# Transposing on VectorE instead of TensorE in a batched product x yᵀ: pair-packed casts, 32x32 block transposes and block-diagonal weights

## The chip, the cores and the metric

The kernel runs on one core of one Trainium2 chip. The metric is the device time of one execution in microseconds; the median of several runs is quoted. The profile of an execution covers a span that is about 2 us shorter than the device time. A run is called slow when it lies over 1.5% above the fastest of the same kernel.

In the profile lines PE is TensorE's matmuls, PEld its weight loads, DVE VectorE, ACT ScalarE and POOL GpSimd; q1 is the queue of the kernel's DMAs, q8 and q14 are the queues that the page calls "instruction". A packet of a load or an output is one contiguous row (the 24 loads of the kernel before, of 256 rows of 4 KB each, are 6144 packets of 4 KB).

## The reference

```python
batch, n_heads, seq_t, seq_s, channels = 8, 12, 512, 512, 64
# x: (8, 12, 512, 64) float32, y: (8, 12, 512, 64) float32
np.einsum('bhtc,bhsc->bhts', x, y)        # out: (8, 12, 512, 512) float32
```

There are 96 heads. Each is a product of a 512x64 and a 64x512 matrix. Inputs are 25.17 MB, the output is 100.66 MB: the kernel mostly writes.

## The kernel before

It takes 8 heads per group and has 12 groups. POOL casts the inputs to bf16, TensorE transposes them (128x128 against an identity), VectorE and ACT copy the transposes out of PSUM, TensorE multiplies with 64x64 weights, ACT and VectorE evict 128x1024 blocks into an output tile of 2 MB, and one DMA writes each tile. The parts that matter here:

```python
xv = x...rearrange("(g a p n) -> g p a n", a=2, p=P, n=R * C)   # rows of 4 KB, two per partition
lpool bufs=3, opool bufs=6 ...
def load(g):
    nc.sync.dma_start(ys..., yv[g]); nc.sync.dma_start(xs..., xv[g])
def prepare(g, made):                     # in steps, amid the matmuls of group g - 1
    ... nc.gpsimd.tensor_copy(b[:, rows], s[:, :, rows]...)     # 4 casts of 128x1024
    if g + AHEAD < NG: load(g + AHEAD)
    ... nc.tensor.transpose(pt[:, k, :], yb[...], ident)        # 32 per group
    ... nc.vector.tensor_copy(dst, src) / nc.scalar.activation(dst, src, COPY)
# cut: loops over groups, head pairs and k
for two in range(2):
    for h in range(2):
        nc.tensor.matmul(pm[h * 64:(h + 1) * 64, two, :], xT[...64 columns...], yT[...512 columns...])
if k % 2 == 0: nc.scalar.activation(ot[...], pm, COPY)
else:          nc.vector.tensor_copy(ot[...], pm)
# 2 MB per output DMA; at the two ends of the run in halves of 1 MB
nc.sync.dma_start(ov[g, 2 * a + pair], otf)
```

## Time and profile before

| | before |
|---|---|
| device time, median | 306.41 us (306.17 to 306.41, its first 3 runs) |
| span of the profile | 304.3 us |
| instructions on PE and PEld | 2304 |
| 16 KB instruction fetches (queue q8) | 9 |
| DMA packets of data | 6144 of 4 KB, 1024 of 8 KB, 5632 of 16 KB |
| last compute | 277.6 us |

The prediction below shows the main lines. Two more groups of that page are what the change removes (line, engine, operation, output and input, count; busy time and mean nanoseconds; idle time ahead of it and its releaser):

```profile
L126 PE MATMUL pm<-yT,xT 64*64 64x512 bf16 x768 | 164.0, 610 | 56.0 <-ACT ot L133 53.9
...
L82 PE MATMUL pt<-ident,yb 128*128 128x128 bf16 x192 | 23.7, 307 | 10.7 <-POOL yb L73 6.9
```

The second appears twice, for yb and xb. The page's chain of waits has PE in 23% of the span, most of that before 63 us, where PE is busy nearly all the time. But the DMA row is at 9 there too, and later the matmuls wait for ACT, and ACT for output DMAs. So this time should not set the end.

A word that the document uses throughout: each DMA leaves 16 completion increments in the trace (1216 for the 76 DMAs of the kernel before), and the page counts 16 DMA engines. One increment is read as the end of one engine's part; the times fit this, as 16 packets of 159 ns, a sixteenth of a load of 1 MB, take 2.54 us, and the first increments of two such loads are 2.56 us apart. The **spread** of a DMA is the time from its first increment to its last. It tells how far the slowest engine lags the fastest. No view of the profile prints it; it was computed from the increments in the trace.

### The profile page before, as it was taken

The numbers are of one execution on the slowest core, as the hardware profiler recorded it, in microseconds if no ns is written. First come the engines' busy times: TensorE is split into PE (matmuls) and PEld (weight loads), VectorE is DVE, ScalarE is ACT, GpSimd is POOL, SyncE is SP. The second block draws the span as 40 slices with busy tenths as digits, with TensorE's granted clock in tenths as the row PEclk, the third lists the DMA queues.
The fourth block names the chain that finished last, engine by engine and source line by source line (L and its number), as shares of the span: only waits on it lengthen the run. The fifth ranks groups of instructions, "written<-read, shape, count | busy, mean of one in ns | idle before, by whom it ended". The sixth has DMA issues, their size and how long they took to land.

```text
span 304.3 us, 2968 instructions
## 1 busy us (share of the span) xinstructions
PE 208.5 (69%) x1152; PEld 104.6 (34%) x1152; DVE 144.7 (48%) x120; ACT 119.4 (39%) x121; POOL 49.3 (16%) x54
## 2 busy tenths in 40 slices
PE   0899999999959538928946844893897797671000
PEld 0444344555425114513613522541453443330000
DVE  0456666567446435616525733743565664443000
ACT  1454645364445224624515512542364552522000
POOL 3773220400500310230050050031000000000000
PEclk9999999999999855555555655555555555555555
DMA  7999999999999999999999999999999999999992
GB/s 283 411 410 418 436 429 423 419 442 405 445 419 419 430 431 421 420 437 424 426 426 435 414 429 433 413 433 429 433 433 429 431 433 429 428 428 433 423 420 89
DMA packets 14031, 126.03 MB, mean 414 GB/s; under 512 B 1216, under 2 KB 1216, under 8 KB 7360
## 3 DMA queue, kind: packets, MB, share of 16 engines
q1 hardware_dynamic: 14016, 125.83, 98.2%
q8 instruction: 9, 0.15, 0.2%
q14 instruction: 6, 0.05, 0.0%
HBM read 25.17 MB, written 100.66 MB: 413 GB/s over the span
## 4 chain that ended last, share of the span: by engine, by line
DMA 60%; PE 23%; DVE 4%; ACT 2%; issue 1%; POOL 1%; SPq 0%; ACTq 0%
DMA out_dram<-ot 48%; PE pm L126 17%; DMA xs<-in_x_dram 12%; PE pt L82 3%; PE pt L96 3%; DVE ot L135 2%; ACT ot L133 2%; DVE xT L102 1%; POOL xb L73 1%; SPq L55 0%; ACTq L133 0%; SPq L140 0%; ACT xT L104 0%; SPq L56 0%
## 5 line engine op out<-in xcount | busy, mean ns | idle before, releaser
L126 PE MATMUL pm<-yT,xT 64*64 64x512 bf16 x768 | 164.0, 610 | 56.0 <-ACT ot L133 53.9
L135 DVE COPY ot<-pm 128x1024 f32<-128x1024 f32 x96 | 117.2, 1223 | 113.3 <-PE pm L126 57.3
L133 ACT ACTIVATE ot<-pm 128x1024 f32<-128x1024 f32 x96 | 95.1, 1023 | 113.7 <-DMA out_dram<-ot 81.2
L126 PEld LDWEIGHTS <-xT 64*64 64x64 bf16 x768 | 66.1, 150 | 131.2 <-issue 122.7
L73 POOL CAST yb<-ys 128x1024 bf16<-128x1024 f32 x24 | 24.3, 1040 | 140.5 <-DMA ys<-in_y_dram 94.7
L82 PE MATMUL pt<-ident,yb 128*128 128x128 bf16 x192 | 23.7, 307 | 10.7 <-POOL yb L73 6.9
L73 POOL CAST xb<-xs 128x1024 bf16<-128x1024 f32 x24 | 24.3, 1040 | 16.3 <-issue 6.9
L82 PEld LDWEIGHTS <-yb 128*128 128x128 bf16 x192 | 19.9, 143 | 20.3 <-issue 11.5
L96 PE MATMUL pt<-ident,xb 128*128 128x128 bf16 x192 | 24.9, 310 | 1.1 <-POOL xb L73 0.9
L96 PEld LDWEIGHTS <-xb 128*128 128x128 bf16 x192 | 19.1, 141 | 19.3 <-issue 17.8
L104 ACT ACTIVATE xT<-pt 128x1024 bf16<-128x1024 bf16 x12 | 12.3, 1024 | 32.9 <-PE pt L96 29.4
L102 DVE COPY xT<-pt 128x1024 bf16<-128x1024 bf16 x12 | 14.7, 1223 | 10.8 <-PE pt L96 9.4
L88 DVE COPY yT<-pt 128x1024 bf16<-128x1024 bf16 x12 | 14.6, 1216 | 8.9 <-PE pt L82 8.9
L90 ACT ACTIVATE yT<-pt 128x1024 bf16<-128x1024 bf16 x12 | 12.3, 1022 | 9.3 <-PE pt L82 7.7
L90 ACT ACT_TABLE_LOAD x1 | 1.3, 1283 | 0.7 <-PEq L155 0.7
masks.py:199 POOL TENSOR_SCALAR_AFFINE_SELECT ident<-ident 128x128 bf16<-128x128 bf16 x1 | 0.3, 292 | 0.1
masks.py:197 POOL MEMSET ident<- 128x128 bf16 x1 | 0.2, 204 | 0.3 <-POOLq L155 0.3
L155 POOL MEMSET const-float32-0.0<- 128x1 f32 x1 | 0.1, 98 | 0.2 <-issue 0.2
L155 POOL MEMSET const-bfloat16-1.0<- 128x1 bf16 x1 | 0.1, 101 | 0.0
L155 POOL MEMSET const-uint8-127<- 128x1 uint8 x1 | 0.1, 101 | 0.0
L155 POOL MEMSET const-float32-1.0<- 128x1 f32 x1 | 0.1, 98 | 0.0
## 6 DMA issues: line engine op xcount, KB each, us to landing
out_dram<-ot SPq DMA_DIRECT2D x44, 2048.0 KB, 28.3
ys<-in_y_dram SPq DMA_DIRECT2D x12, 1024.0 KB, 20.3
xs<-in_x_dram SPq DMA_DIRECT2D x12, 1024.0 KB, 22.2
out_dram<-ot SPq DMA_DIRECT2D x8, 1024.0 KB, 21.0
```

What stands on the lines that cost most here:

```text
L73: nc.gpsimd.tensor_copy(b[:, rows], s[:, :, rows].rearrange("p a r c -> p r a c"))
L82: nc.tensor.transpose(pt[:, k, :], yb[:, half * K + k].rearrange("p a c -> p (a c)"), ident)
L88: nc.vector.tensor_copy(dst, src)
L90: nc.scalar.activation(dst, src, COPY)
L96: nc.tensor.transpose(pt[:, k, :], xb[:, e * K + half * K // 2 + i].rearrange("p a c -> p (a c)"), ident)
L102: nc.vector.tensor_copy(dst, src)
L104: nc.scalar.activation(dst, src, COPY)
L126: nc.tensor.matmul(pm[h * 64:(h + 1) * 64, two, :], xT[a * C:(a + 1) * C, 2 * k + two, col:col + Q].rearrange("c n e -> c (n e)"), yT[a * ...
L133: nc.scalar.activation(ot[:, 2 * k:2 * k + 2, :], pm, COPY)
L135: nc.vector.tensor_copy(ot[:, 2 * k:2 * k + 2, :], pm)
L155: nc = _bacc.Bacc("TRN2", target_bir_lowering=False, num_devices=1)
```

## The change

Its intent is to take the transposes away from TensorE, and with them the copies out of PSUM. The casts arrange channel halves in partition blocks of 32 and pack two values per 32-bit element; VectorE transposes 32x32 blocks of such elements; weights become 128x128 blocks that are block-diagonal over two heads (the zeros are written once). Each partition now loads 8 KB in one piece, and every output is a DMA of 2 MB. Cut to its core:

```diff
-    xv = ....rearrange("(g a p n) -> g p a n", a=2, p=P, n=R * C)
-    ov = ....rearrange("(g a p n) -> g a p n", a=4, p=P, n=K * S)
+    xv = ....rearrange("(g p n) -> g p n", p=P, n=R * C)
+    ov = ....rearrange("(o u h q n) -> o h q u n", u=2, h=2, q=Q * E, n=K * S)
-    opool ... bufs=6
+    opool ... bufs=7
-            nc.gpsimd.tensor_copy(b[:, rows], s[:, :, rows].rearrange("p a r c -> p r a c"))
+    # six casts per half group on POOL, each of 32 or 64 partitions
+    cast(engines[n % len(engines)], xv2[(2 * ch + u) * D:(2 * ch + u + 1) * D, :, :, :, u], ...)
-            nc.tensor.transpose(pt[:, k, :], yb[...], ident)      # 384 in all, and 48 copies
+    nc.vector.transpose(xT..., xb...)                              # 24 of 128x1024 uint32
+    nc.vector.transpose(yT..., yb...)                              # 24 of 128x512 uint32
-    nc.tensor.matmul(pm[h * 64:(h + 1) * 64, two, :], <64 columns>, ...)      # 768
+    nc.tensor.matmul(pm[:, two, :], xT[:, k + two, h, :], yT[:, h * S:(h + 1) * S], ...)   # 384
+    if step == 12 and g + AHEAD < NG:
+        load(g + AHEAD)                                            # just ahead of the group's last tile
+    if k == 4: nc.vector.tensor_copy(...)                          # else ACT: 3 of 4 evictions
```

More of the change, by code (lines that the diff above doesn't have):

```diff
@@ L6 @@
 from concourse._compat import with_exitstack
-from concourse.masks import make_identity
 @with_exitstack
@@ L26 @@
     P = 128
-    G = 4
+    G = 8
     Q = P // G
     R = T // Q
-    NG = B * H // (2 * G)
-    K = R // 2
+    NG = B * H // G
+    K = 8
+    E = R // K
+    D = 32
     AHEAD = 3
@@ L34 @@
     bf16 = mybir.dt.bfloat16
+    u32 = mybir.dt.uint32
     COPY = mybir.ActivationFunctionType.Copy
-    assert C * 2 == P and S == T and R == 16
-    xv = x.rearrange("b h t c -> (b h t c)").rearrange("(g a p n) -> g p a n", a=2, p=P, n=R * C)
-    yv = y.rearrange("b h t c -> (b h t c)").rearrange("(g a p n) -> g p a n", a=2, p=P, n=R * C)
-    ov = out.rearrange("b h t s -> (b h t s)").rearrange("(g a p n) -> g a p n", a=4, p=P, n=K * S)
+    assert C == 2 * D and S == T and R == D and Q * 2 == D
@@ L42 @@
+    xv = x.rearrange("b h t c -> (b h t c)").rearrange("(g p n) -> g p n", p=P, n=R * C)
+    yv = y.rearrange("b h t c -> (b h t c)").rearrange("(g p n) -> g p n", p=P, n=R * C)
+    ov = out.rearrange("b h t s -> (b h t s)").rearrange(
+        "(o u h q n) -> o h q u n", u=2, h=2, q=Q * E, n=K * S
+    )
     const = ctx.enter_context(tc.tile_pool(name="const", bufs=1))
     lpool = ctx.enter_context(tc.tile_pool(name="lpool", bufs=AHEAD))
-    bpool = ctx.enter_context(tc.tile_pool(name="bpool", bufs=2))
@@ L45 @@
-    tpool = ctx.enter_context(tc.tile_pool(name="tpool", bufs=2))
-    opool = ctx.enter_context(tc.tile_pool(name="opool", bufs=6))
-    ptpool = ctx.enter_context(tc.tile_pool(name="ptpsum", bufs=2, space=bass.MemoryType.PSUM))
-    pmpool = ctx.enter_context(tc.tile_pool(name="pmpsum", bufs=3, space=bass.MemoryType.PSUM))
-    loaded = {}
+    ybpool = ctx.enter_context(tc.tile_pool(name="ybpool", bufs=2))
+    tpool = ctx.enter_context(tc.tile_pool(name="tpool", bufs=4))
+    opool = ctx.enter_context(tc.tile_pool(name="opool", bufs=7))
@@ L52, in load @@
+    pmpool = ctx.enter_context(tc.tile_pool(name="pmpsum", bufs=4, space=bass.MemoryType.PSUM))
+    loaded, made = {}, {}
+    zeroed = [const.tile([P, K * E * D], u32, name=f"xb{half}") for half in range(2)]
     def load(g):
-        xs = lpool.tile([P, 2, R, C], fp32)
-        ys = lpool.tile([P, 2, R, C], fp32)
-        nc.sync.dma_start(ys.rearrange("p a r c -> p a (r c)"), yv[g])
-        nc.sync.dma_start(xs.rearrange("p a r c -> p a (r c)"), xv[g])
+        xs = lpool.tile([P, R, C], fp32)
+        ys = lpool.tile([P, R, C], fp32)
+        nc.sync.dma_start(xs.rearrange("p r c -> p (r c)"), xv[g])
+        nc.sync.dma_start(ys.rearrange("p r c -> p (r c)"), yv[g])
@@ L57, in load @@
         loaded[g] = (xs, ys)
-    for g in range(AHEAD):
-        load(g)
-    ident = const.tile([P, P], bf16)
-    make_identity(nc, ident)
-    def prepare(g, made):
-        xs, ys = loaded.pop(g)
-        yb = bpool.tile([P, R, 2, C], bf16)
-        xb = bpool.tile([P, R, 2, C], bf16)
-        for s, b in ((ys, yb), (xs, xb)):
-            for half in range(2):
-                rows = slice(half * K, (half + 1) * K)
-                nc.gpsimd.tensor_copy(b[:, rows], s[:, :, rows].rearrange("p a r c -> p r a c"))
-        if g + AHEAD < NG:
-            load(g + AHEAD)
-        yield
-        yT = tpool.tile([P, G * Q, R], bf16)
-        xT = tpool.tile([P, K, P, 2], bf16)
-        for half in range(2):
-            pt = ptpool.tile([P, K, P], bf16)
-            for k in range(K):
-                nc.tensor.transpose(
-                    pt[:, k, :], yb[:, half * K + k].rearrange("p a c -> p (a c)"), ident
-                )
-            dst = yT[:, :, half * K:(half + 1) * K]
-            src = pt.rearrange("p k n -> p n k")
-            if half == 0:
-                nc.vector.tensor_copy(dst, src)
-            else:
-                nc.scalar.activation(dst, src, COPY)
-            yield
-        for half in range(2):
-            pt = ptpool.tile([P, K, P], bf16)
-            for k in range(K):
-                e, i = divmod(k, K // 2)
-                nc.tensor.transpose(
-                    pt[:, k, :], xb[:, e * K + half * K // 2 + i].rearrange("p a c -> p (a c)"), ident
-                )
-            dst = xT[:, half * K // 2:(half + 1) * K // 2]
-            src = pt.rearrange("p (e i) n -> p i n e", e=2)
-            if half == 0:
-                nc.vector.tensor_copy(dst, src)
-            else:
-                nc.scalar.activation(dst, src, COPY)
-            yield
-        made[g] = (xT, yT.rearrange("p n k -> p (n k)"))
@@ L108 @@
-    made = {}
-    for _ in prepare(0, made):
-        pass
-    for g in range(NG):
-        xT, yT = made.pop(g)
-        steps = prepare(g + 1, made) if g + 1 < NG else iter(())
-        for a in range(2):
-            for pair in range(2):
-                ot = opool.tile([P, K, S], fp32)
-                otf = ot.rearrange("p r s -> p (r s)")
-                edge = (g == 0 and a == 0) or (g == NG - 1 and a == 1)
-                for k in range(K // 2):
-                    if (pair * K // 2 + k) in (0, 3, 6):
-                        next(steps, None)
-                    pm = pmpool.tile([P, 2, S], fp32)
-                    for two in range(2):
-                        for h in range(2):
-                            col = (2 * pair + h) * Q
-                            nc.tensor.matmul(
-                                pm[h * 64:(h + 1) * 64, two, :],
-                                xT[a * C:(a + 1) * C, 2 * k + two, col:col + Q].rearrange("c n e -> c (n e)"),
-                                yT[a * C:(a + 1) * C, (2 * pair + h) * S:(2 * pair + h + 1) * S],
-                                start=True, stop=True,
-                            )
-                    if k % 2 == 0:
-                        nc.scalar.activation(ot[:, 2 * k:2 * k + 2, :], pm, COPY)
-                    else:
-                        nc.vector.tensor_copy(ot[:, 2 * k:2 * k + 2, :], pm)
-                    if edge and k % 2 == 1:
-                        i, j = (2 * k - 2) * S, (2 * k + 2) * S
-                        nc.sync.dma_start(ov[g, 2 * a + pair][:, i:j], otf[:, i:j])
-                if not edge:
-                    nc.sync.dma_start(ov[g, 2 * a + pair], otf)
@@ new lines, in cast, with casts @@
+    def cast(engine, dst, src):
+        if engine is nc.scalar:
+            nc.scalar.activation(dst, src, COPY)
+        else:
+            engine.tensor_copy(dst, src)
+    def casts(g, half, engines):
+        xs, ys = loaded[g]
+        xb = zeroed[half]
+        xv2 = xb.bitcast(bf16).rearrange("p (k e c u) -> p k e c u", k=K, e=E, u=2)
+        base = half * 64
+        n = 0
+        for ch in range(2):
+            for u in range(2):
+                lo = base + u * D
+                src = xs[lo:lo + D, :, ch * D:(ch + 1) * D]
+                cast(
+                    engines[n % len(engines)],
+                    xv2[(2 * ch + u) * D:(2 * ch + u + 1) * D, :, :, :, u],
+                    src.rearrange("p (e k) c -> p k e c", k=K),
+                )
+                n += 1
+        yb = ybpool.tile([P, R // 2 * D], u32)
+        yv2 = yb.bitcast(bf16).rearrange("p (j c w) -> p j w c", j=R // 2, w=2)
+        for ch in range(2):
+            cast(
+                engines[n % len(engines)],
+                yv2[ch * 64:(ch + 1) * 64],
+                ys[base:base + 64, :, ch * D:(ch + 1) * D].rearrange("p (j w) c -> p j w c", w=2),
+            )
+            n += 1
+        return xb, yb
@@ new lines, in transposes @@
+    def transposes(g, half, xb, yb):
+        xT = tpool.tile([P, K * D * E], u32)
+        nc.vector.transpose(
+            xT.rearrange("p (k r e) -> p k e r", k=K, e=E),
+            xb.rearrange("p (k e c) -> p k e c", k=K, e=E),
+        )
+        yT = tpool.tile([P, D * R // 2], u32)
+        nc.vector.transpose(
+            yT.rearrange("p (r j) -> p j r", r=D), yb.rearrange("p (j c) -> p j c", c=D)
+        )
+        made[g, half] = (
+            xT.bitcast(bf16).rearrange("p (k h m) -> p k h m", k=K, h=2), yT.bitcast(bf16)
+        )
@@ new lines, in result @@
+    def result(g, half, h, steps):
+        xT, yT = made[g, half]
+        ot = opool.tile([P, K, S], fp32)
+        for k in range(0, K, 2):
+            next(steps, None)
+            pm = pmpool.tile([P, 2, S], fp32)
+            for two in range(2):
+                nc.tensor.matmul(
+                    pm[:, two, :], xT[:, k + two, h, :], yT[:, h * S:(h + 1) * S], start=True, stop=True
+                )
+            if k == 4:
+                nc.vector.tensor_copy(ot[:, k:k + 2, :], pm)
+            else:
+                nc.scalar.activation(ot[:, k:k + 2, :], pm, COPY)
+        nc.sync.dma_start(ov[2 * g + half, h], ot.rearrange("p r s -> p (r s)"))
@@ new lines, in prepare @@
+    def prepare(g):
+        b = {}
+        for step in range(16):
+            if step in (0, 1):
+                b[step] = casts(g, step, [nc.gpsimd])
+            if step in (5, 13):
+                transposes(g, step // 8, *b[step // 8])
+            if step == 12 and g + AHEAD < NG:
+                load(g + AHEAD)
+            yield
+    with tc.manual_schedule():
+        for g in range(AHEAD):
+            load(g)
+        nc.vector.memset(zeroed[0], 0.0)
+        nc.gpsimd.memset(zeroed[1], 0.0)
+        b0 = casts(0, 0, [nc.vector, nc.scalar, nc.gpsimd])
+        transposes(0, 0, *b0)
+        b1 = casts(0, 1, [nc.gpsimd, nc.scalar])
+        transposes(0, 1, *b1)
+        if AHEAD < NG:
+            load(AHEAD)
+        for g in range(NG):
+            steps = prepare(g + 1) if g + 1 < NG else iter(())
+            for half in range(2):
+                for h in range(2):
+                    result(g, half, h, steps)
+            for _ in steps:
+                pass
```

## The prediction

> **What bounds the kernel now.** I read the page's engine totals first, then the slices, the windows, the end of the run, the DMA packets and the DMA landings. No compute engine is near full, while the DMA row is full from the second slice to the last but one:
>
> ```profile
> PE 208.5 (69%) x1152; PEld 104.6 (34%) x1152; DVE 144.7 (48%) x120; ACT 119.4 (39%) x121; POOL 49.3 (16%) x54
> ...
> DMA  7999999999999999999999999999999999999992
> ...
> q1 hardware_dynamic: 14016, 125.83, 98.2%
> q8 instruction: 9, 0.15, 0.2%
> ```
>
> Kernel data alone takes 98.2% of all 16 engines' time. The waits say the same from the other side: the evictions wait for an output tile to be written out, not the DMA for the evictions.
>
> ```profile
> L135 DVE COPY ot<-pm 128x1024 f32<-128x1024 f32 x96 | 117.2, 1223 | 113.3 <-PE pm L126 57.3
> L133 ACT ACTIVATE ot<-pm 128x1024 f32<-128x1024 f32 x96 | 95.1, 1023 | 113.7 <-DMA out_dram<-ot 81.2
> ...
> L73 POOL CAST yb<-ys 128x1024 bf16<-128x1024 f32 x24 | 24.3, 1040 | 140.5 <-DMA ys<-in_y_dram 94.7
> ```
>
> Compute ends at 277.6 us and the DMA drains for 25 us more. So compute speed, transposes on TensorE and PE's half clock are all hidden, and only three things can move the time: bytes (unchanged: 25.17 MB in, 100.66 MB out), the cost per packet, and how evenly the 16 engines finish. The last is visible in the table of windows (columns: stretch, its length, busy of PE, PEld, DVE, ACT, POOL, clock, DMA share, GB/s):
>
> ```profile
> 290.00:296.00 6.00, 0.00 (x0) 0.00 (x0) 0.00 (x0) 0.00 (x0) 0.00 (x0) 0.50 1.00 425
> 296.00:300.00 4.00, 0.00 (x0) 0.00 (x0) 0.00 (x0) 0.00 (x0) 0.00 (x0) 0.50 0.47 197
> 300.00:302.00 2.00, 0.00 (x0) 0.00 (x0) 0.00 (x0) 0.00 (x0) 0.00 (x0) 0.50 0.14 57
> 302.00:304.30 2.30, 0.00 (x0) 0.00 (x0) 0.00 (x0) 0.00 (x0) 0.00 (x0) 0.50 0.03 14
> ```
>
> From 296 us on most engines are done, and for the last microseconds about one engine works (a share of 0.03 to 0.14 of 16 engines). That straggler sets the end.
>
> **Packets and landings.** The trace has every DMA packet. By size, the median durations are: 4096 B (6144 packets, all loads) 159 ns; 8192 B (1024, the small outputs at the edges) 309 ns; 16384 B (5632, the other outputs) 611 ns. So a packet costs some 8 ns beside its bytes. Each DMA also has 16 completion increments, one per engine. The interval of one DMA to the next at the first increment is 2.56 us for a 1 MB load, 2.45 us for a 1 MB output and 4.86 us for a 2 MB output. 24 x 2.56 + 8 x 2.45 + 44 x 4.86 = 294.9 us: the time of the fastest engine. The spread from first to last increment of one DMA grows: 0.47 us at 23 us into the span, 1.8 at 28, 2.3 at 53, 3.0 at 80, 3.9 at 115, 4.4 at 130, 5.2 at 180, 6.7 at 269, 6.6 at the end. Its steps fall mostly just after the nine 16 KB packets of the q8 instruction queue, which start at 23.3, 49.0, 73.8, 100.8, 132.4, 170.8, 200.9, 231.9 and 265.6 us and take 0.9 to 1.1 us each. The one at 200.9 left no step, and part of the growth from 224 to 264 us is gradual, so this is a reading and not proof. On average (6.58 - 0.47) / 9 = 0.68 us per fetch.
>
> The account closes: first packet at 1.83 us, 294.9 us of the fastest engine, 6.1 us of added skew, the last landing at 303.2, the end at 304.3 us.
>
> [...]PE and PEld together are 2304 instructions, 9 x 256, and there are nine 16 KB packets, one each 128 or so weight loads.[...] No run here shows one yet; I take the trace's [...]copy (1.22 us for 1024) in its place.
> [...]The trace has only VectorE reads of PSUM, beside which every x cast stayed at 1.04 us.
>
> **The change part by part.**
> (1) Input packets. Each partition now takes 8 KB from one place instead of two of 4 KB: 3072 packets for 6144. I take the 8 KB output packet's 309 ns for a read. One engine has 16 x 160 ns = 2.56 us per load now, and 8 x 309 = 2.47 us after; 24 x 0.09 = 2.1 us less.
> (2) Output packets. All 48 outputs are of 2 MB: 48 x 4.86 = 233.3 us instead of 19.6 + 213.8 = 233.4 us: nothing. Rows now alternate between two heads 2 MB apart, still 16 KB each; I assume no cost.
> (3) Instructions. The 384 transposes on PE go, and 768 64-row matmuls become 384 of 128x128: PE and PEld fall from 2304 to 768 instructions, three blocks in place of nine. Six fetches less at 0.68 us are 4.1 us less skew on the last engine. The short 8 KB fetches of the other queues (six in the run, 309 ns each) stay about as many, as ACT and POOL get more instructions and DVE fewer.
> (4) Compute, hidden if it stays below the DMA's 294.9 us. ACT: 144 evictions x 1.023 = 147 us. DVE: 48 x 1.223 = 59 us, plus per half group one transpose of 1024 elements (1.22)[...]. POOL: 6 casts per half of 1024 elements each, on a quarter or half of the partitions, whose time I take as that of 128: 24 x 6 x 1.04 = 150 us. PE: 8 matmuls of 512 columns per tile; now 16 of the paired kind take 3.6 us at half clock, and 8 full ones should take the same: 48 x 3.5 = 170 us. All are under 60%. An output tile that comes free is refilled in 3 x 1.02 us on ACT while six others are queued (6 x 4.86 = 29 us).
> (5) The start. x0 lands near 5.8 us and y0 near 8.4 as y0 and x0 do now. Casts on three engines, transposes, then ACT's casts of the second half to 12.5, evictions to 15.6: first output at 15.7 us. It was 16.0, of half the size. Four loads (the fourth is issued at 12.6) keep the DMA busy to 1.8 + 8 x 2.47 = 21.6 us. Output 2 waits behind POOL's casts of group 1 (12.6 + 6.2 = 18.8) and the transposes, about 22 us, while output 1 keeps the DMA to 26.5. So no gap, with some 4 us to spare.
> Sum: 306.4 - 2.1 - 4.1 = 300.2 us. I put it at 300.5, as some of the skew is not tied to fetches and mishaps only add.
>
> **The rivals.**
> A, the same bytes, the same time: the straggler is slow for a reason of its own, not by fetches. For it: the gradual growth and the fetch without a step. Then only part (1) remains: 304.3 us.
> B, POOL becomes the bound. Its casts now write 2-byte elements at 4-byte steps and shift partitions; nothing in the profile shows such a cast. At 2.1 us each they take 25 us per group, against 2 x 2.47 + 4 x 4.86 = 24.4 us of DMA, and the start opens a gap of 5 us or more: about 310 us. At 3 us, 36 us a group: some 440. Against it: the present cast reads its rows in pieces and still takes 1.02 ns an element.
> C, the two-head output rows or the other split of rows over the engines slow the writes. A 5% longer 2 MB output costs 48 x 0.24 = 12 us: 312. Nothing in the profile speaks for it but that all the present outputs are contiguous.
> D, the transposes are several times slower than a copy. In the steady state still hidden; at the start output 1 comes some 6 to 10 us later, and the DMA idles 1 to 4 us: 302 to 304.
>
> **Range and chances.** Without mishap I expect 299 to 302: (1) is 1.5 to 2.3 us, (3) is 2.5 to 5. Threshold for 2% is 300.3, in the middle of this. A and D give 302 to 304.5, one chance in four. B and C, one in ten, give over 308. Predicted 300.5, range 298.7 to 305.5; faster by over 2% 0.42, within 2% 0.50, slower 0.08.
>
> **What would show it.** Right: read packets of 8192 B near 309 ns; three 16 KB instruction packets; a spread of the last landing of 2 to 3 us; DMA row at 9 throughout; POOL near 150 us with 1.04 us casts. Wrong: POOL casts of 2 us and output tiles that wait for them; 16 KB packets over 620 ns; a dip of the DMA row in the slices from 15 to 45 us; a spread that stays over 5 us although fetches are fewer.

Where the text is marked as cut, passages are left out that no trace or run of this case shows. The fetches in (3) rest on the count: 2304 instructions on PE and PEld and nine packets of 16 KB, 256 instructions each. "No run here shows one yet" speaks of a transpose on VectorE: the 1.22 us of one of 1024 elements in (4) are the author's estimate, from the copy of that size in the trace.

## The result, and the profile after

The changed kernel is correct and takes 304.56 us (304.17 to 305.03, 4 runs) against 306.41 us (306.17 to 306.89, 4 runs). The ratio is 0.9939, with a 95% interval of 0.992 to 0.9957. Ratios here are the mean time of one kernel's fast runs over that of the other's of the same rounds, so they are not quite the ratio of the medians. The verdict is "same" (within 2%), with a gain of 1.85 us where 5.9 us was forecast. The time lies in the stated range, but the forecast gain was three times too large.

Totals, slices and queues of the page after:

```profile
PE 138.1 (46%) x384; PEld 46.9 (15%) x384; DVE 130.8 (43%) x99; ACT 145.0 (48%) x150; POOL 182.2 (60%) x142
...
DMA  7999999999999999999999999999999999999993
...
q1 hardware_dynamic: 10368, 125.83, 98.2%
q8 instruction: 3, 0.05, 0.1%
q14 instruction: 6, 0.05, 0.0%
```

The DMA row is as full as it was, the packets of q1 fell from 14016 to 10368 (data alone: from 12800 to 9216), and the fetches on q8 from nine to three: what was counted came true. The end of the run, in the table of windows with the columns as in the prediction:

```profile
290.00:296.00 6.00, 0.00 (x0) 0.00 (x0) 0.00 (x0) 0.00 (x0) 0.00 (x0) 0.50 1.00 429
296.00:300.00 4.00, 0.00 (x0) 0.00 (x0) 0.00 (x0) 0.00 (x0) 0.00 (x0) 0.50 0.34 143
300.00:302.00 2.00, 0.00 (x0) 0.00 (x0) 0.00 (x0) 0.00 (x0) 0.00 (x0) 0.50 0.04 16
```

The share between 296 and 300 us fell only from 0.47 to 0.34, and a last engine still works after 300 us. The same, read from the increments of the last DMA:

```
                 first engine    last engine    spread
before            296.63 us       303.20 us     6.57 us
after             296.72 us       301.86 us     5.14 us
```

So two readings of the forecast fail at once: the fastest engine is not 2.1 us earlier but as late as before, and the spread is not 2 to 3 us but 5.1, one of the signs that the prediction had named for being wrong.

The new groups, all hidden beside the DMA:

```profile
L128 ACT ACTIVATE ot<-pm 128x1024 f32<-128x1024 f32 x144 | 137.0, 1028 | 120.0 <-DMA out_dram<-ot 103.0
L70 POOL CAST xb<-xs 32x1024 bf16<-32x1024 f32 x91 | 120.4, 1323 | 49.6 <-DMA xs<-in_x_dram 31.1
...
L70 POOL CAST yb<-ys 64x1024 bf16<-64x1024 f32 x46 | 60.6, 1318 | 3.3 <-DMA ys<-in_y_dram 0.5
L102 DVE STREAM_TRANSPOSE xT<-xb 128x1024 uint32<-128x1024 uint32 x24 | 49.4, 2057 | 13.2 <-POOL xb L70 11.6
L107 DVE STREAM_TRANSPOSE yT<-yb 128x512 uint32<-128x512 uint32 x24 | 24.9, 1038 | 5.7 <-POOL yb L70 5.7
```

The evictions still wait for output DMAs (103.0 us of ACT's 120.0 idle). A cast (1.32 us) and a transpose of 1024 elements (2.06 us) are slower than forecast (1.04 and 1.22 us), without consequence.

### The profile page after: what moved, and what is told of

Read it like the earlier page. It is cut to its first block, busy times and chain, and to the rows that moved or that the text cites. A ratio compares the mean times of both kernels' runs of the same rounds, so it can differ in the third digit from the quotient of the medians.

```text
span 302.7 us, 1551 instructions
## 1 busy us (share of the span) xinstructions
PE 138.1 (46%) x384; PEld 46.9 (15%) x384; DVE 130.8 (43%) x99; ACT 145.0 (48%) x150; POOL 182.2 (60%) x142
## 3 DMA queue, kind: packets, MB, share of 16 engines
q1 hardware_dynamic: 10368, 125.83, 98.2%
## 4 chain that ended last, share of the span: by engine, by line
DMA 75%; POOL 10%; ACT 2%; issue 1%; DVE 0%; ACTq 0%; PE 0%; SPq 0%; POOLq 0%
DMA out_dram<-ot 62%; DMA ys<-in_y_dram 12%; POOL xb L70 6%; POOL yb L70 4%; ACT ot L128 2%; DVE ot L126 0%; PE pm L122 0%; ACTq L186 0%; SPq L62 0%; POOLq L70 0%; ACTq L128 0%; SPq L129 0%; DVE yT L107 0%; SPq L63 0%
## 5 line engine op out<-in xcount | busy, mean ns | idle before, releaser
L122 PE MATMUL pm<-yT,xT 128*128 128x512 bf16 x384 | 138.1, 514 | 128.9 <-ACT ot L128 95.8
L128 ACT ACTIVATE ot<-pm 128x1024 f32<-128x1024 f32 x144 | 137.0, 1028 | 120.0 <-DMA out_dram<-ot 103.0
L70 POOL CAST xb<-xs 32x1024 bf16<-32x1024 f32 x91 | 120.4, 1323 | 49.6 <-DMA xs<-in_x_dram 31.1
L126 DVE COPY ot<-pm 128x1024 f32<-128x1024 f32 x48 | 58.1, 1215 | 115.0 <-DMA out_dram<-ot 108.7
L122 PEld LDWEIGHTS <-xT 128*128 128x128 bf16 x384 | 46.9, 122 | 219.2 <-issue 194.9
L70 POOL CAST yb<-ys 64x1024 bf16<-64x1024 f32 x46 | 60.6, 1318 | 3.3 <-DMA ys<-in_y_dram 0.5
L102 DVE STREAM_TRANSPOSE xT<-xb 128x1024 uint32<-128x1024 uint32 x24 | 49.4, 2057 | 13.2 <-POOL xb L70 11.6
L107 DVE STREAM_TRANSPOSE yT<-yb 128x512 uint32<-128x512 uint32 x24 | 24.9, 1038 | 5.7 <-POOL yb L70 5.7
L68 ACT ACTIVATE xb<-xs 32x1024 bf16<-32x1024 f32 x3 | 4.0, 1348 | 0.1
L68 ACT ACTIVATE yb<-ys 64x1024 bf16<-64x1024 f32 x2 | 2.7, 1348 | 0.1
## 6 DMA issues: line engine op xcount, KB each, us to landing
xs<-in_x_dram SPq DMA_DIRECT2D x12, 1024.0 KB, 26.7
ys<-in_y_dram SPq DMA_DIRECT2D x12, 1024.0 KB, 26.7
```

The lines of the kernel that those rows point to most:

```text
L70: engine.tensor_copy(dst, src)
L102: nc.vector.transpose(xT.rearrange("p (k r e) -> p k e r", k=K, e=E), xb.rearrange("p (k e c) -> p k e c", k=K, e=E),)
L107: nc.vector.transpose(yT.rearrange("p (r j) -> p j r", r=D), yb.rearrange("p (j c) -> p j c", c=D))
L122: nc.tensor.matmul(pm[:, two, :], xT[:, k + two, h, :], yT[:, h * S:(h + 1) * S], start=True, stop=True)
L126: nc.vector.tensor_copy(ot[:, k:k + 2, :], pm)
L128: nc.scalar.activation(ot[:, k:k + 2, :], pm, COPY)
```

## The experiments

After the result two theories stood against each other, and the expectations name them.
**Theory 1** is the prediction's: nearly all of the spread comes from instruction fetches, 0.68 us each, and each 4 KB load packet costs its fixed price everywhere.
**Theory 2**: a fetch holds up one engine, not always the late one; the spread comes mainly from loads, at the turn from a group of loads to the next outputs; and the fixed price of a load packet hardly shows amid outputs.
"The changed kernel" in the runs below is at a ratio of 0.9939 (first measurement) or 0.995 (repeated). Differences are taken against the first unless said otherwise; against the repeat they shift by 0.3 us, and differences from the changed kernel are known to some 0.5 to 0.7 us at best. Spreads are those of one profiled run each.

### More instruction blocks, the same DMAs

```diff
-    nc.tensor.matmul(pm[:, two, :], xT[:, k + two, h, :], yT[:, h * S:(h + 1) * S], ...)
+    for n in range(4):
+        nc.tensor.matmul(pm[:, two, n * P:(n + 1) * P], xT[:, k + two, h, :],
+                         yT[:, h * S + n * P:h * S + (n + 1) * P], ...)
```

> The changed kernel with every matmul of 512 columns split into four of 128, each with its own weight load: 3072 PE instructions instead of 768, so 12 blocks of 16 KB instead of 3; same DMA traffic, PE still hidden. Theory 1 (the prediction's: all fetches burden the same, last engine, 0.68 us each): 9 x 0.68 = 6.1 us slower than the changed kernel, about 310.5 us, spread of the last DMA over 10 us. Theory 2 (each fetch holds up one engine by about 1.3 us, but another engine each time, and the last engine is late by stalls of load packets): 0 to 1.5 us slower, 304.5 to 306 us, while the mean end of the 16 engines comes about 9 x 1.3 / 16 = 0.7 us later.

The 1.3 us of Theory 2 are the author's assumption; the nearest that a trace shows is a step of the spread by 1.2 us, with the fetch at 61.6 us in the changed kernel.

Measured: 307.16 us, correct, ratio 1.0011 (0.9999 to 1.0023). Against the changed kernel that is 0.0072 x 306.6 = 2.2 us for nine more fetches, 0.25 us each (1.9 us, 0.21 each, against the repeat). Its queue line and the end of its run:

```profile
q8 instruction: 12, 0.20, 0.2%
```

```profile
296.00:300.00 4.00, 0.00 (x0) 0.00 (x0) 0.00 (x0) 0.00 (x0) 0.00 (x0) 0.50 0.42 180
300.00:302.00 2.00, 0.00 (x0) 0.00 (x0) 0.00 (x0) 0.00 (x0) 0.00 (x0) 0.50 0.08 33
302.00:304.00 2.00, 0.00 (x0) 0.00 (x0) 0.00 (x0) 0.00 (x0) 0.00 (x0) 0.50 0.06 25
```

In 302 to 304 us a share of 0.06, about one engine, is at work: the last engine ends 7.97 us after the first, the second last 4.49 us after it. Fetches are not free, and they are worth about a third of what the prediction gave them. Theory 2's "0 to 1.5 us" was too small too; its other sign came half true, the mean end of the 16 engines being 0.45 us later (298.59 for 298.14 us) where it had 0.7. So the nine fetches held up several engines, and the last one most.

### Three blocks fewer in the kernel before

```diff
-    for h in range(2):
-        col = (2 * pair + h) * Q
-        nc.tensor.matmul(pm[h * 64:(h + 1) * 64, two, :], <64 columns of xT>, <yT of head h>, ...)
+    col = 2 * pair * Q
+    nc.tensor.matmul(pm[:, two, :], <128 columns of xT>, <yT of the first head>, ...)
```

> Wrong result on purpose: the kernel before with one 128-column weight matmul in place of each pair of 64-column ones (the second head's rows are not its own): 1536 PE instructions, 6 fetched blocks in place of 9, the DMA traffic unchanged. By the prediction's 0.68 us a block: 2.0 us faster than before, 304.5 us. By e1_pe_x4's 2.2 us for nine blocks, 0.25 us each: 0.7 us faster, 305.8 us.

Measured: 305.23 us, wrong, ratio 0.9956 (0.9944 to 0.9969), 1.3 us faster, with a last spread of 5.54 us for 6.57 and six fetches:

```profile
q8 instruction: 6, 0.10, 0.1%
```

That is 0.45 us a block (0.32 to 0.57 by the interval), between the two expectations. Together the two runs bracket a block at 0.25 to 0.45 us, so the six blocks that the change saves are worth 1.5 to 2.7 us. The change gained 1.85 us in all. (This edit also halves the number of product matmuls; PE's busy time hardly moved, 206.2 us for 208.5.)

### The size of load packets, in both kernels

In the changed kernel, two DMAs of 4 KB rows for each tensor:

```diff
-    nc.sync.dma_start(xs..., xv[g]); nc.sync.dma_start(ys..., yv[g])
+    for t, v in ((xs, xv), (ys, yv)):
+        for i in range(2):
+            w = slice(i * R * C // 2, (i + 1) * R * C // 2)
+            nc.sync.dma_start(t...[:, w], v[g][:, w])
```

> The changed kernel with each input tensor of a group loaded by two DMAs of 4 KB rows instead of one of 8 KB rows: 6144 load packets again. Theory 1 (every 4 KB packet costs its 8 ns also amid the outputs): 2.1 us slower, 306.7 us. Theory 2 (the price is only seen in the first eight loads, where nothing but loads is in flight; amid outputs it is hidden): 8 x 0.08 = 0.6 us slower, 305.2 us.

Measured: 305.05 us, correct, ratio 0.9944 (0.993 to 0.9959), 0.15 us slower than the changed kernel, no clear difference. Its packets, 6144 of them of 4 KB:

```profile
DMA packets 13834, 125.94 MB, mean 415 GB/s; under 512 B 1536, under 2 KB 1536, under 8 KB 7680
```

In the kernel before, 8 KB rows (the rows reach wrong partitions, so the result is wrong):

```diff
-    ....rearrange("(g a p n) -> g p a n", a=2, p=P, n=R * C)
+    ....rearrange("(g p n) -> g p n", p=P, n=2 * R * C)
```

> Wrong result on purpose (rows reach the wrong partitions): the kernel before with its loads taken as 8 KB rows, 3072 load packets instead of 6144, all else as it was. This is the first part of the change alone. Theory 1: 2.1 us faster than before, 304.3 us. Theory 2: gain only in the ten loads ahead of the first output, 10 x 0.08 = 0.8 us, 305.6 us.

Measured: 306.60 us, ratio 0.9989 (0.9977 to 1.0001), 0.3 us faster, and not clear of zero. Both runs refute the 2.1 us of Theory 1. The first part of the change, alone, gives 0 to 0.7 us.

```profile
DMA packets 10959, 126.03 MB, mean 414 GB/s; under 512 B 1216, under 2 KB 1216, under 8 KB 1216
```

### The DMAs without the compute

Casts, transposes, matmuls and evictions are gone; the loads keep their places in the order, and memsets fill the output tiles:

```diff
-    <casts, transposes, matmuls, evictions>
+    nc.vector.memset(ot[:, 0:K // 2, :], 1.0)
+    nc.gpsimd.memset(ot[:, K // 2:K, :], 1.0)
     nc.sync.dma_start(ov[2 * g + half, h], ot...)
```

> Wrong result on purpose: the changed kernel's loads and outputs in their order, without casts, transposes, matmuls and evictions; output tiles are filled by memsets. No PE blocks are fetched. Theory 1 (fetches make the last engine late): the spread of the last DMA falls to about 0.5 us, 298.5 us. Theory 2 (load packets that stall amid outputs make it late): spread still 3 to 5 us, 302 to 304 us. Either way this is the floor of this stream of DMAs.

Measured: 303.66 us, ratio 0.989 (0.9875 to 0.9906). This is the most telling run. With no PE instruction at all, hence no fetch on q8, the end looks as it did (the columns are now only DVE and POOL, then clock, DMA share, GB/s):

```profile
q1 hardware_dynamic: 10368, 125.83, 98.4%
q14 instruction: 3, 0.02, 0.0%
```

```profile
290.00:296.00 6.00, 0.00 (x0) 0.00 (x0) 1.00 1.01 431
296.00:300.00 4.00, 0.00 (x0) 0.00 (x0) 1.00 0.32 135
300.00:302.00 2.00, 0.00 (x0) 0.00 (x0) 1.00 0.04 16
```

The spread of its last DMA is 5.10 us, as in the changed kernel (5.14). (This profile is of the slowest of its four runs, 304.19 us; the fastest took 302.79, so the spread differs from run to run.) After the first turn from loads to outputs, where it rises from 0.29 to 0.70 us, it grows lastingly only at the eight pairs of loads that stand amid outputs. The change of the spread from the output ahead of a pair to the output after it, in three kernels (the table gives the time at which the pair's first load begins to land, and the growth in us):

```
DMA only (no q8)      40: 0.46   65: 0.30   89: 1.06   114: 1.09   138: 0.65   162: 0.90   187: 0.46   211: 0.31
changed kernel        40: 0.26   65: 0.74   89: 0.38   114: 0.83   138: 0.09   163: 0.84   187: 0.06   212: 0.66
kernel before         50: 0.80   75: 0.68   99: 0.91   123: 0.41   148: 0.01   172: 0.87   197: 0.00
```

Most of the growths are overstated, by up to 0.3 us, as the spread of the output just ahead of a pair often dips: in the DMA-only kernel they add up to 5.2 us for a lasting 4.4. The DMA-only kernel still has three 8 KB fetches on q14, one at 170.1 and two at 193.3 us; of its eight growths only the one at 187 us may be theirs. After its last load, at 214 us, the DMA-only kernel's spread stays at 5.10 us for the remaining 17 outputs. This is the confusion behind the prediction: in the kernel before, fetches start at 49.0, 73.8, 100.8, 170.8 and 200.9 us, each within 4 us of a pair of loads. What was read as the mark of the fetch was in large part the mark of the loads: nine blocks at the 0.25 to 0.45 us measured above are 2.3 to 4.0 us (an estimate) of the 6.1 us that were given to them. The run also sets the floor: all compute of the changed kernel, its three fetches included, costs (0.9939 - 0.989) x 306.6 = 1.5 us over its bare DMAs.

### The outputs without the loads

```diff
-    load(...)      # all removed from the DMA-only kernel
```

> Wrong result on purpose: the DMA-only kernel without its loads, 48 outputs of 2 MB back to back. Theory 2 (engines fall behind where a group of loads turns into outputs): the spread stays at its first value, under 0.6 us, from the first DMA to the last; 1.8 + 48 x 4.86 + 0.5 + 1.1 = 236.7 us of span, some 238.7 us. Rival 3 (some engines are slower at moving data, whatever it is): the spread grows in proportion to the bytes, by about 5 x 100.7/125.8 = 4 us to the end, 242 us.

Measured: 243.31 us, with a spread of 0.33 us at the last output. The spread decides: it does not grow in proportion to the bytes, so Rival 3 falls, although its time of 242 us is close. (That the DMA-only kernel's spread stays at 5.10 us over its last 17 outputs says the same.) Theory 2's "under 0.6 us from the first DMA to the last" did not hold: at 142 us two 8 KB instruction fetches on q14 start, and the spread jumps to 1.17 us. It then shrinks again, as the late engine takes 4.87 us per output and the first one 4.91. So with outputs alone a late engine catches up, which it does not do in the DMA-only kernel. Of the 4.6 us over Theory 2's time, about half is a later start (the first packet waits for the first memsets, 4.4 us instead of 1.8) and about half the outputs themselves: one per 4.91 us on average rather than 4.86. The second half of its run in the table of windows, with the columns of the DMA-only kernel:

```profile
120.00:240.00 120.00, 32.11 (x19) 32.48 (x18) 1.00 1.01 427
```

Why the outputs run 1% slower when all engines keep in step stays open (the median 16 KB packet takes 615 ns here and 611 in the DMA-only kernel).

### Loads in pairs of groups

```diff
-    lpool bufs=AHEAD, opool bufs=7
+    lpool bufs=AHEAD + 1, opool bufs=6
-    if step == 12 and g + AHEAD < NG:
-        load(g + AHEAD)
+    if step == 12 and g % 2 == 1:
+        for later in (g + AHEAD, g + AHEAD + 1):
+            if later < NG: load(later)
     # and all of the first AHEAD + 1 groups are loaded at the start
```

> The changed kernel with the loads of two groups issued together (four load buffers for three, six output tiles for seven): loads turn into outputs 5 times in place of 9; packets and bytes are the same. Theory 2 (each such turn costs the last engine some 0.45 us): 4 x 0.45 = 1.8 us faster than the changed kernel, 302.7 us, and a spread of about 3.5 us. Rival 4 (each load packet amid outputs has its own chance to stall): no change, 304.5 us.

Measured: 304.07 us, correct, ratio 0.9918 (0.9905 to 0.9932). As this overlaps the changed kernel's interval, both were run again on one chip:

> The changed kernel once more, as the neighbour of the next two: 304.5 us, ratio 0.993 to 0.995.

> The changed kernel with paired loads once more: if the gain of e7_load_pairs is real, ratio 0.991 to 0.993, 0.4 to 0.8 us under the changed kernel of the same call; if it was chance, the two agree within 0.2 us.

Measured: the changed kernel 305.13 us, ratio 0.995 (0.9938 to 0.9962); paired loads 304.07 us again, ratio 0.9918 (0.9906 to 0.9931). The intervals are apart: (0.995 - 0.9918) x 306.5 = 1.0 us. The gain over the changed kernel is real, 0.6 us in the first comparison and 1.0 in the second, but not the 1.8 us of Theory 2. (The edit also has one load buffer more and one output tile fewer; this was not separated.) The last spreads are 4.84 and 4.43 us, not 3.5: in the first profile the turn at 138 us alone raised the spread by 2.09 us instead of 0.45, and between 204 and 272 us the spread grew by some 0.08 us with each output although no loads were in flight. That slow growth, which the repeat and, from 224 to 264 us, the kernel before also show, is unexplained. There the last engine does write more slowly than the first (4.94 us per output for 4.86).

### Loads on a second ring

By a ring the expectation means the queue of DMAs of one issuing engine. Here the loads get one of their own.

```diff
-    nc.sync.dma_start(xs..., xv[g]); nc.sync.dma_start(ys..., yv[g])
+    nc.scalar.dma_start(xs..., xv[g]); nc.scalar.dma_start(ys..., yv[g])
```

> The changed kernel with the loads issued from ACT's queue[...]. Theory 2 as a turn of the ring: no sharp turn any more, so the steps of the spread go or shrink, 302 to 303 us. Rival 4: each load packet still meets outputs, now all of them do: 304.5 us or slower.

Measured: 305.19 us, correct, ratio 0.9955 (0.9943 to 0.9968), no better than the changed kernel; the last spread is 6.24 us. The two rings are seen as two queues, and a load of x lands 11.9 us after its issue (median), where it took 26.7 us in the changed kernel:

```profile
q1 hardware_dynamic: 6912, 100.67, 77.8%
q10 hardware_dynamic: 3456, 25.17, 20.1%
```

So Theory 2's picture of a sharp turn is not the whole: on a queue of their own, loads cost as much (Rival 4's reading). What is shown is that with the loads the spread comes (5.10 us at the end of the DMA-only kernel) and without them it does not last (0.33 us), and that in the DMA-only kernel it grows where loads stand. What in a load packet makes an engine late is not shown, nor what makes the spread creep up amid outputs in the paired kernel (1.2 us).

### Which engines are late

The trace does not number the engines. It shows the increments of tiny loads behind the last output: one of n rows leaves n + 1 increments, one of them 0.4 to 1.6 us after its issue, long before the others. As n falls, one of the late times after another drops out of the list. The one that drops out between n + 1 and n rows is called **position** n here, and is read as the end of the last output on one engine. That a position is the same engine in each run and kernel is the author's assumption; no run shows it. Where the expectations number engines, these are positions.

```diff
+    for n in range(15, 0, -1):          # second pair of runs: (12, 8, 7, 6, 5, 4, 3, 2, 1)
+        nc.sync.dma_start(probe[:n], xf[0:n, 0:16])
```

> The changed kernel with 15 tiny loads (64 bytes a row, 15 rows down to 1) after the last output. [...]If the late engines are always the same ones (theory 2: loads burden certain engines), this probe and that of the kernel before name the same two or three; if the lateness is chance or follows the instruction fetches, they differ. Time within 1 us of the changed kernel plus about 1 us for the tiny loads.

> The same probe after the last output of the kernel before. Theory 2: the same late engines as in the changed kernel. Chance or fetches: others.

> The changed kernel with tiny loads of 12, 8, 7, 6, 5, 4, 3, 2 and 1 rows after the last output[...]. If lateness belongs to fixed engines, engines 12 and 13 are late again by 3 to 6 us, and one engine under 9 is late by some 5 us.

> The same for the kernel before: engine 12 late by some 6 us, and the same low-numbered engine as in the changed kernel if lateness belongs to fixed engines.

Measured (single runs, correct; 308.39, 310.29, 306.54 and 307.89 us: the first expectation of the time was a miss, why was not tested; only the increments of the tiny loads are used). End of the last output by position, in us of the span (the second probes don't tell the order within 12 to 15):

```
                         position 12 13       14       15       the last one under 9     most others
changed, first probe      301.92    300.44   298.52   299.32    302.16                   296.8 to 297.6
before, first probe       303.18    300.58   299.82   297.24    304.00                   296.8 to 299.4
changed, second probe     12 to 15: 302.28, 301.72, 300.65, 299.73    position 4: 300.76 296.4 to 297.4
before, second probe      12 to 15: 303.44, 300.62, 300.33, 297.55    position 4: 303.62 296.8 to 299.2
```

In both kernels the late ones are position 4 (300.76 and 303.62 us) and three or four of positions 12 to 15. The same positions are late in whichever kernel, which speaks against chance; if a position is one engine, as assumed, fixed engines are late. What makes them late (engine, partition or address in the loads) was not tested. That it also speaks against the fetches was the expectation's assumption: no run shows which engine carries a fetch, so against them as the main cause stands the DMA-only run (5.10 us with no fetch on q8).

### The slower casts and transposes

```diff
-    xv2[..., u]                              # every second bf16 of the tile
+    xv3[..., u]                              # dense rows: tile seen as (u k e c)
-    xT.rearrange("p (k r e) -> p k e r", ...)
+    xT.rearrange("p (k e r) -> p k e r", ...)
```

> Wrong result on purpose: the changed kernel with the x casts writing dense 2-byte rows in place of every second 2-byte element, and the x transposes writing 32 adjacent elements in place of a step of 16 bytes. If the 4-byte step is what raised a POOL cast from 1.04 to 1.32 us, the x casts here take about 1.04 us; if the 32-partition shift or the source rows of 32 elements do, they stay at 1.32. The 1024-element transpose [...]falls if the step did it. The time stays within 0.5 us of the changed kernel in either case, as both are hidden.

The other side of the last alternative is cut, as it named a rate that no run shows: the transpose was to stay at 2.06 us if the 32-bit transpose itself, not the step, made it slow.

Measured in one look (304.58 us, wrong as intended; 304.58 was also a time of the changed kernel):

```profile
L70 POOL CAST xb<-xs 32x1024 bf16<-32x1024 f32 x91 | 94.5, 1039 | 73.5 <-DMA xs<-in_x_dram 49.8
...
L103 DVE STREAM_TRANSPOSE xT<-xb 128x1024 uint32<-128x1024 uint32 x24 | 29.7, 1237 | 6.9 <-POOL xb L70 6.6
```

The cast returns to 1.04 us and the transpose to 1.24 us. It was the step of the destination that made the one a quarter and the other two thirds slower, not the move between partitions nor the 32-bit transpose. It is no matter of POOL alone: the same x casts on ACT fell from 1.35 to 1.05 us and on DVE from 1.24 to 1.06.

## Why the prediction was right or wrong

- **What bounds the kernel: right.** The DMA row stayed at 9, evictions still wait for outputs, and PE's busy time fell by 70 us without effect. The bare DMAs alone need 303.66 us. One reading was off: not one engine but two were last, 6.49 and 6.57 us after the first (a share of 0.14 of 16 engines is two).
- **(1) Input packets, -2.1 us: wrong, and the step is the term of the sum that was mis-sized.** It measured 0.15 us (undoing it) and 0.3 us (doing it alone, interval 0 to 0.7). The prediction took the rate of the first eight loads, 2.56 us each, for all 24. Those have only loads beside them. Amid outputs two loads and an output take 9.83 us on the fastest engine before and 9.78 after; counted from one output earlier, so that any delay of the output ahead of the loads is included, it is 14.73 and 14.76 us: nothing is left of the 0.09 us a load. The first seven loads did gain 0.08 us each (2.48 against 2.56), but the eighth took 2.94 us and so gave most of it back; why it stalled was not tested. The median of the 8 KB read packets is 309 ns as assumed, but their mean is 322.
- **(2) Output packets, nothing: right.** 16 KB packets stay at 611 ns with rows that alternate between two heads, so rival C fell.
- **(3) Fetches, -4.1 us: the count was right, the size wrong.** Nine became three, for 768 instructions on PE and PEld: 256 each, as before. The step that failed is "(6.58 - 0.47) / 9 = 0.68 us per fetch": it gave all growth of the spread to the fetches. Without any fetch on q8 the spread still grows to 5.10 us. The trace before held a warning besides the fetch at 200.9 us: the step to 4.37 us was there at 130.4 us, ahead of the fetch at 132.4. A block is worth 0.25 to 0.45 us at the end, 1.5 to 2.7 us for six, enough for nearly all of the 1.85 us that was gained. The growth in the changed kernel shows why the price varies: the fetch at 61.6 us raises the spread by 1.2 us, those at 146.5 and 246.0 us leave it as it was. PE itself hardly felt them: it was busy for 37.5 of the 38 us from 22 to 60 us in the kernel before, in which two fetches fall.
- **(4) Compute: hidden, as said, with sizes off.** ACT 145 us for 147. POOL 182 for 150 (1.32 us a cast), DVE 131 (58 in evictions, for 59; 2.06 us a transpose of 1024 elements instead of 1.22, 1.04 us one of 512), PE 138 for 170 (its granted clock was 0.718 on average, above the half clock of the estimate). All stay at 60% or less, so rival B, with casts of 2 us, did not come about, nor rival D: the transposes are 1.7 times as slow as a copy and stay hidden.
- **(5) The start: right.** The first output was issued at 16.8 us instead of 15.7, and the DMA row shows no empty slice (in slices of 1 us it dips to 0.7, first at 21 us).
- **Rival A** named the right kind of failure (a straggler with a reason of its own) and 304.3 us. Its number came close partly by luck: it kept the 2.1 us of (1), which failed, and dropped all of (3), which is what was gained.

The chances were spread evenly about the 2% line; the point estimate leaned on a correlation that one run without compute would have broken.

## What to carry to other kernels

This kernel is bound by its DMAs (98.2% of the time of 16 engines, before and after), and its last engine, 5.14 to 6.57 us after the first, sets the time. In such a case look at how far apart the engines end before crediting anything to packet size or compute. Instruction blocks cost this kernel 0.25 us (nine added, 2.2 us) to 0.45 us (three removed, 1.3 us) each, so fewer and larger matmuls paid a little although TensorE was not the limit. Two things that recur at the same interval cannot be told apart in one trace: take one of them away.
